# SSD entry of a hybrid trunk layer: the decay clamps' engine, the z gate's buffer, and the places of the gate product and of the later output-weight splits

## The chip, the cores and the metric

The kernel runs on one core of one Trainium2 chip. The metric is the device time of one launch in microseconds (us), the median of three runs. The engines are named as the profile names them: PE is the matrix engine TensorE, with PEld for its weight loads, DVE is VectorE, ACT is ScalarE, POOL is GpSimd, and SP is SyncE, which only issues transfers here.

## What is computed

One layer of a streaming encoder: 1024 tokens, width 1024, all in float32. The normalised input goes through one projection; its columns feed an SSD (Mamba-2) group of 8 heads and an attention group of 8 heads; the two outputs side by side go through the output projection, and a feed-forward block follows. The change touches the SSD group alone:

```python
def ssd_scan(xdt, adt, bm, cm):
    ...
    a_cs = jnp.cumsum(A, axis=2)
    seg = a_cs[:, :, :, None] - a_cs[:, :, None]
    causal = jnp.tril(jnp.ones((L, L), dtype=bool))[:, :, None, None]
    decay_ls = jnp.exp(jnp.where(causal, seg, -jnp.inf))
    cb = jnp.einsum('bclgn,bcsgn->bclsg', Cm, Bm)
    y_diag = jnp.einsum('bclsg,bclsge,bcsgep->bclgep', cb, decay_ls, X)
    ...
def ssd_mixer(z, xbc, dt_raw, conv_w, conv_b, dt_bias, a_log, d_skip, norm_w):
    ...
    y = ssd_scan(xs * dt[..., None], dt * A, bm, cm)
    y = y + d_skip.astype(jnp.float32)[:, None] * xs
    y = y.reshape(b, s, SSD_WIDTH) * jax.nn.silu(z.astype(jnp.float32))
    return rmsnorm(y, norm_w).astype(z.dtype)
```

`seg` is the difference of two running sums, the exponent of a decay. The kernel clamps it at zero before the exponential, so that positions outside the causal triangle, which a mask sets to zero afterwards, cannot overflow. `z` is the gate: its silu multiplies the SSD output.

## The kernel before

**Matrix products.** Every float32 operand of a large product is kept as a high and a low half, and each product is three matmuls (`mm3`, L77 to L79). The halves are made by `split` (L81 to L87): the high half on ScalarE (L83 with a scale, L86 without), then the low half, the operand minus its high half, on VectorE (L84, L87).

**What sets the order.** A scheduler places every instruction in the queue of its engine by its own estimate of time; the engines then work through their queues in order. `tc.issue_after(i)` adds one constraint: what is issued under it comes behind `i` in the queue of `i`'s own engine. It says nothing about other engines. TensorE's order in the SSD loop is written out in this way by `pe` (L706 to L710), which puts each matmul behind the one before it.

**The z projection.** `z_tile` (L640) makes the gate for one tile of 128 tokens, 260 columns at a time; `wz_weights` loads the weights of one pass. The pass `ch == 1` comes first, then `ch == 0` for tiles 0 to 7. In the second pass ScalarE's tanh goes from PSUM into the buffer `zt`, of which there is one (L655), and VectorE's product of that and the PSUM tile goes into `zs` (L656). Tiles 2 to 5 of this pass lie in the two PSUM banks `s`, the others in `acc` and `pv` (named `zps`). `zlast` keeps the tanh and the product of the last tile.

**Output weights.** `wout_split` halves the eight blocks of output weights. Blocks 0 to 3 go into `hth[0]`/`htl[0]` during the second z pass. Blocks 4 to 7 go into `hth[1]`/`htl[1]`, the memory that token tiles 4 to 7 of the layer's normalised input occupy until the z matmuls have read them. Each is scaled by column halves, so four blocks make eight instructions L83 (tile `hH1`) and eight L84 (tile `hL1`). They are issued behind both entries of `pin`.

**The SSD loop.** The 1024 tokens are eight chunks of 128. For each, `ssd_pre` (L712) prepares:
- `xdt` on VectorE (L716) and `xdd` on GpSimd (L717);
- the gate's fine factor, an in-place product on `zs` on GpSimd (L719);
- the decay exponents `cr`, running sums fetched by a transfer from DRAM to all partitions, with two buffers;
- the clamps, one for each head: heads 0 to 3 on ScalarE (L726), heads 4 to 7 on VectorE (L728);
- `cb` on VectorE from TensorE's products (L737), the exponential `th` of four heads on ScalarE (L743), and `th` times `cb` on VectorE (L744).

Chunk 0's share of this is issued during the z pass, behind its tile 0; each later chunk's stands in the iteration of the chunk before it. `ssd_y` (L807) then runs TensorE's products: `ydp` (from `xdt` and `th`), `yop` from the state, and `stp` for the next state; VectorE sums them into `yy` (L832). `ssd_norm` (L838) multiplies `yy` by the gate (L840), squares it on ScalarE (L842), takes the root of the mean on GpSimd (`rstd`, L118), and scales on ScalarE (L844). `ssd_turn` (L846) transposes `yy` on TensorE into `xps`. `wout_half` (L875) runs the output projection (`wops`) of the chunk, part of it between the loop's other steps.

PSUM is handed over when the z pass ends: the pools that hold `s`, `acc` and `pv` close, and `ydp`, `yop`, `stp` (tag `ssd`), `xps` and `wops` open in their banks. Chunk 0's `ydp` gets the bank of z tile 5.

The loop as written:

```python
    for c in range(NT):
        if c == 1:
            ssd_turn(*turn)
        y, t = ssd_y(c, *pre)
        if c > 1:
            ssd_turn(*turn)
        if c == 1:
            at = wout_rhs(0, 1)
        if c > 1:
            ssd_norm(c, y, t)
        turn = (c, y)
        if c < NT - 1:
            pre = ssd_pre(c + 1, x_tile, lambda: wout_half(c, slice(0, 3)))
            if c < 2:
                ssd_norm(c, y, t, at)
            row_scale(pin[0])
            wout_half(c, slice(3, 8))
            if c == 0:
                for j in range(4, 8):
                    pin[:] = zlast
                    wout_split(j, wt[j])
        else:
            wout_half(c)
```

Of the kernel before, what the change touches and what calls it, by code (L numbers as in the profile page):

```python
# [10 lines left out]
F32 = mybir.dt.float32  # L11
# [54 lines left out]
def tile_block(ctx: ExitStack, tc: tile.TileContext, x, crep, pk, w_ada, w_first, w_ft, w_z,  # L66
# [573 lines left out]
    def z_tile(ch, st, wz):  # L640
# [4 lines left out]
        for kt in range(KT):  # L645
            mm3(ps, hth[st // 4][:, st % 4, kt, :], htl[st // 4][:, st % 4, kt, :],
                wz[kt // 2][0][:, kt % 2, :],
                wz[kt // 2][1][:, kt % 2, :], kt == 0, kt == KT - 1)
        nz = 260
        if ch == 1:  # L650
            A.activation(zs[:, st, 260:512], ps[:, 0:252], AF.Silu)
            V.tensor_tensor(zs[:, st, 512:520], ps[:, 252:260], pkt[:, DTB:DTB + 8], ALU.add)
            return
        th = wzp.tile([P, 272], F32, tag="zt", bufs=1, name="zt")
        zlast[:] = [A.activation(th[:, 0:nz], ps[:, 0:nz], AF.Tanh).ins,  # L655
                    V.scalar_tensor_tensor(zs[:, st, ch * 260:ch * 260 + nz], th[:, 0:nz], 1.0, ps[:, 0:nz],  # L656
                                           op0=ALU.add, op1=ALU.mult).ins]

# [53 lines left out]
    def ssd_pre(c, xp_, between=None):  # L712
# [5 lines left out]
        ms_ = []  # L718
        G.tensor_tensor(h8(zs[:, c, 0:512]), h8(zs[:, c, 0:512]), hb("t", c), ALU.mult)  # L719
        cr = bcp.tile([P, 8, P], F32, tag="rm", bufs=2, name="cr")  # L720
        nc.sync.dma_start(cr, rows_from(acd, 8 * c, 8))
        for g in range(2):
            for k in range(4 * g, 4 * g + 4):
                a = acc_[:, 8 * c + k:8 * c + k + 1]
                if g == 0:
                    A.activation(cr[:, k], cr[:, k], AF.Relu, scale=-1.0, bias=a)  # L726
                else:
                    V.tensor_scalar(cr[:, k], cr[:, k], a, 0.0, op0=ALU.subtract, op1=ALU.min)  # L728
            if g == 0:
# [12 lines left out]
            m = th512().rearrange("p (h l) -> p h l", h=4)  # L742
            pin1 = A.activation(m, cr[:, 4 * g:4 * g + 4], AF.Exp, scale=(-1.0, 1.0)[g])  # L743
            pin2 = V.tensor_tensor(m, m, cb[:, g:g + 1, :].to_broadcast([P, 4, P]), ALU.mult)  # L744
            ms_.append(m)
        pin[:] = [pin1.ins, pin2.ins]
        return xdt, xdd, cb, ms_

# [58 lines left out]
    def ssd_y(c, xdt, xdd, cb, ms_):  # L807
# [28 lines left out]
        return y, t  # L836

    def ssd_norm(c, y, t, at=None):  # L838
        with tc.issue_after(at) if at else ExitStack():
            V.tensor_tensor(y, y, zs[:, c, 0:512], ALU.mult)  # L840
        ms = stat()
        A.activation(t, y, AF.Square, accum_out=ms)  # L842
        r = rstd(ms, 512.0 * EPS)
        A.activation(y, y, AF.Copy, scale=r)  # L844
# [93 lines left out]
    for c in range(NT):  # L938
# [10 lines left out]
        if c < NT - 1:  # L949
# [5 lines left out]
            if c == 0:  # L955
                for j in range(4, 8):
                    pin[:] = zlast
                    wout_split(j, wt[j])
# [610 lines left out]
```

## Time and profile before

| | |
|---|---|
| runs | 1210.37, 1210.83, 1214.28 us |
| median | 1210.83 us |
| profiled execution | 1213.89 us |
| its span, first to last instruction | 1212.2 us |
| mean granted TensorE clock | 0.991 |
| PEld, weight loads | 970.0 us busy (80%) |
| DVE | 930.4 us (77%) |
| ACT | 579.5 us (48%) |
| POOL | 159.0 us (13%) |

A row of a timeline gives the start in us from the span's start, the duration, the engine, the line of the kernel, the operation, the tiles written and read, the shape and the count of equal instructions in a row; in brackets stands the wait ahead of it and what ended it. A row of the windows gives the stretch and its length, then the busy time of TensorE (with its number of instructions), weight loads, VectorE, ScalarE and GpSimd, then TensorE's mean granted clock (1.00 is full speed), the DMA engines' share and GB/s. A row of the waits gives the group that waited, the engine, tile and line that released it, the sum, the count and the longest. In the page's chain, each engine's share is that of the chain of work that ended last.

### The profile page before, as it was taken

Reading aid. Unit: us, or ns where it says so; the run is one execution under the profiler, and the core shown is the slowest. Engines: PE = TensorE matmul, PEld = TensorE weight load, DVE = VectorE, ACT = ScalarE, POOL = GpSimd, SP = SyncE. Lnnn points to the kernel's source line nnn. Section 1 sums busy time; section 2 is a strip of 40 time slices with the busy share of each in tenths; the row PEclk is TensorE's granted clock in tenths of the full one; section 3 lists DMA queues with packets and bytes.
Section 4 is the critical chain, followed back from the end, with each engine's and each line's share of the span. In section 5 each row is a group of like instructions: output and inputs, shape, how many; then the busy total and the mean of one; then the engine's idle time right before and its main releaser. Section 6 shows DMA issues by size and latency. Waiting matters only on the chain.

```text
span 1212.2 us, 15576 instructions
## 1 busy us (share of the span) xinstructions
PE 1161.0 (96%) x5767; PEld 970.0 (80%) x5767; DVE 930.4 (77%) x1418; ACT 579.5 (48%) x938; POOL 159.0 (13%) x182
## 2 busy tenths in 40 slices
PE   4998999989999989999999999999999999999996
PEld 3877787878879978888788888888888888888885
DVE  6846455686596888747999988898889779766986
ACT  4536455673243556476544543345334445433454
POOL 1202232441000255300000000000000000000522
PEclk9999999999999989999999999999999999999999
DMA  9722121311477313141123223322233278733443
GB/s 338 254 59 81 40 64 46 96 73 53 151 255 254 124 36 111 55 148 53 72 102 122 98 107 109 131 78 84 99 131 113 87 269 283 264 116 128 155 132 147
DMA packets 57803, 155.09 MB, mean 128 GB/s; under 512 B 5808, under 2 KB 6016, under 8 KB 56320
## 3 DMA queue, kind: packets, MB, share of 16 engines
q1 hardware_dynamic: 50672, 129.73, 31.4%
q10 hardware_dynamic: 7056, 24.38, 5.1%
q8 instruction: 45, 0.74, 0.2%
q14 instruction: 30, 0.25, 0.1%
HBM read 121.28 MB, written 28.61 MB: 124 GB/s over the span
## 4 chain that ended last, share of the span: by engine, by line
PE 65%; DVE 7%; DMA 2%; ACT 2%; issue 1%; POOL 1%; POOLq 0%; SPq 0%; ACTq 0%; DVEq 0%
PE dn L79 5%; PE dn L78 5%; PE dn L77 5%; PE uY L77 5%; PE uY L79 5%; PE uY L78 5%; PE wops L708 4%; PE uX L79 3%; PE uZ L78 3%; PE uX L77 3%; PE uX L78 3%; PE uZ L77 3%; PE uZ L79 3%; PE s L77 2%; PE s L78 2%; PE s L79 2%
## 5 line engine op out<-in xcount | busy, mean ns | idle before, releaser
L78 PE MATMUL dn<-w 128*128 128x512 f32 x296 | 108.1, 392 | 0.0
L77 PE MATMUL dn<-w 128*128 128x512 f32 x296 | 108.1, 391 | 0.0
L79 PE MATMUL dn<-w 128*128 128x512 f32 x296 | 100.2, 391 | 0.2 <-DVE w L87 0.2
L77 PE MATMUL uY<-tH,w 128*128 128x512 f32 x248 | 97.2, 392 | 0.0
L78 PE MATMUL uY<-tL,w 128*128 128x512 f32 x248 | 97.0, 391 | 0.0
L79 PE MATMUL uY<-tH,w 128*128 128x512 f32 x248 | 96.9, 391 | 0.0
L1430 POOL TENSOR_TENSOR ya<-ya,xs 128x512 f32<-128x512 f32 x4 | 17.2, 4334 | 557.7 <-ACT xs L1426 557.7
L86 ACT ACTIVATE w<-ya 128x1024 fp32r<-128x1024 f32 (+1 forms) x41 | 39.2, 956 | 87.5 <-PE uY L79 84.2
L708 PE MATMUL wops<-hH,yhl 128*128 128x512 f32 x224 | 72.9, 398 | 0.0
L79 PEld LDWEIGHTS dn<-w 128*128 128x128 f32 x296 | 55.4, 188 | 13.2 <-DVE w L87 1.1
L77 PEld LDWEIGHTS dn<-w 128*128 128x128 f32 x296 | 55.5, 188 | 12.4
L78 PEld LDWEIGHTS dn<-w 128*128 128x128 f32 x296 | 55.5, 188 | 12.2
L409 DVE CUSTOM_DVE_ANT_0 p<-s,bias 128x640 f32<-128x640 f32 (+4 forms) x64 | 40.6, 652 | 25.7 <-PE tp L441 10.6
L86 ACT ACTIVATE w<-xs 128x1024 fp32r<-128x1024 f32 (+1 forms) x41 | 39.1, 954 | 38.0 <-PE uY L79 33.3
L415 POOL TENSOR_SCALAR p<-p,st 128x640 f32<-128x640 f32 (+4 forms) x64 | 45.9, 723 | 76.9 <-DVE st L414 66.7
L87 DVE TENSOR_TENSOR pt<-tp,pt 128x512 fp32r<-128x512 f32 (+2 forms) x72 | 42.1, 596 | 17.0 <-ACT pt L86 16.5
L79 PEld LDWEIGHTS uY<-tH,w 128*128 128x128 f32 x248 | 46.5, 188 | 10.4
L77 PEld LDWEIGHTS uY<-tH,w 128*128 128x128 f32 x248 | 46.5, 188 | 10.3
L78 PEld LDWEIGHTS uY<-tL,w 128*128 128x128 f32 x248 | 46.6, 188 | 10.2
L77 PE MATMUL s<-hH,wh 128*128 128x512 f32 x128 | 50.2, 392 | 1.7 <-DVE ct L516 1.7
L1104 DVE SCALAR_TENSOR_TENSOR a<-cv,pkt,a 128x1023 f32<-128x1023 f32 (+1 forms) x40 | 51.1, 1280 | 0.1
L412 ACT ACTIVATE p<-p,st 128x640 f32<-128x640 f32 (+4 forms) x64 | 44.1, 690 | 14.0 <-DVE st L409 13.8
(463 smaller groups left out, 3405.6 us busy)
## 6 DMA issues: line engine op xcount, KB each, us to landing
wos<-in_w_ada_dram SPq DMA_DIRECT2D x25, 512.0 KB, 4.5
gz<-a ACTq DMA_DIRECT2D x10, 1024.0 KB, 5.1
ya<-in_w_up_dram SPq DMA_DIRECT2D x11, 768.0 KB, 4.1
xs<-in_w_up_dram SPq DMA_DIRECT2D x11, 768.0 KB, 4.1
adat<-in_w_ada_dram SPq DMA_DIRECT2D x16, 512.0 KB, 5.8
raws<-in_w_ft_dram SPq DMA_DIRECT2D x14, 512.0 KB, 3.7
gy<-a ACTq DMA_DIRECT2D x10, 512.0 KB, 2.6
qk<-in_x_dram SPq DMA_DIRECT2D x8, 512.0 KB, 7.2
```

Source lines behind the costliest of these rows:

```text
L77: T.matmul(ps, lh, rh, start=start, stop=False, skip_group_check=more)
L78: T.matmul(ps, lh, rl, start=False, stop=False, skip_group_check=more)
L79: T.matmul(ps, ll, rh, start=False, stop=stop, skip_group_check=more)
L86: i = A.activation(hi, src, AF.Copy) if ehi is A else ehi.tensor_copy(hi, src)
L87: return i, elo.tensor_tensor(lo, src, f32(hi), ALU.subtract)
L409: V.tensor_tensor_reduce(out=dst, in0=src, in1=bsl, scale=-1.0, scalar=3e38, op0=ALU.add, op1=ALU.min, accum_out=nm)
L412: A.activation(pv_, pv_, AF.Exp, scale=-1.0, bias=nm, accum_out=rs)
L415: G.tensor_scalar(pv_, pv_, rr, 1.0, op0=ALU.mult, op1=ALU.mult)
L708: i = op(*a, **k)
L1104: V.scalar_tensor_tensor(a[:, j:S], c[:, 0:S - j], w[2 - j], a[:, j:S], op0=ALU.mult, op1=ALU.add)
L1430: G.tensor_tensor(src, src, fnr[:, halves[1]], ALU.mult)
```

## The change

Five things change, all in what `z_tile`, `ssd_pre`, `ssd_norm` and the loop issue.

- The clamps of heads 4 to 7 go to ScalarE with those of heads 0 to 3. They were the minimum of a difference and zero and are now the rectified negative difference, so the sign of their exponential's scale changes with them.
- In the second z pass tanh writes into `zs` itself and the product works there in place; the buffer `zt` is gone. `zlast` holds the product alone.
- The gate's fine product moves from ahead of the clamps to the end of `ssd_pre`, behind the second exponential.
- `ssd_norm` records the gate's product (L840 before) in `gated`.
- Blocks 4 to 7 of the output weights are split behind `zlast` and `gated`. Both entries are VectorE instructions; before, one was the tanh on ScalarE.

```diff
--- before.py
+++ after.py
@@ -646,15 +646,13 @@
             mm3(ps, hth[st // 4][:, st % 4, kt, :], htl[st // 4][:, st % 4, kt, :],
                 wz[kt // 2][0][:, kt % 2, :],
                 wz[kt // 2][1][:, kt % 2, :], kt == 0, kt == KT - 1)
-        nz = 260
         if ch == 1:
             A.activation(zs[:, st, 260:512], ps[:, 0:252], AF.Silu)
             V.tensor_tensor(zs[:, st, 512:520], ps[:, 252:260], pkt[:, DTB:DTB + 8], ALU.add)
             return
-        th = wzp.tile([P, 272], F32, tag="zt", bufs=1, name="zt")
-        zlast[:] = [A.activation(th[:, 0:nz], ps[:, 0:nz], AF.Tanh).ins,
-                    V.scalar_tensor_tensor(zs[:, st, ch * 260:ch * 260 + nz], th[:, 0:nz], 1.0, ps[:, 0:nz],
-                                           op0=ALU.add, op1=ALU.mult).ins]
+        z = zs[:, st, 0:260]
+        A.activation(z, ps[:, 0:260], AF.Tanh)
+        zlast[:] = [V.scalar_tensor_tensor(z, z, 1.0, ps[:, 0:260], op0=ALU.add, op1=ALU.mult).ins]
 
     def dt_prep():
         dtr = zs[:, :, 512:520]
@@ -716,16 +714,12 @@
         V.tensor_tensor(h8(xdt), h8(xs[:, c, :]), hb("dt", c), ALU.mult)
         G.tensor_tensor(h8(xdd), h8(xdt), hb("de", c), ALU.mult)
         ms_ = []
-        G.tensor_tensor(h8(zs[:, c, 0:512]), h8(zs[:, c, 0:512]), hb("t", c), ALU.mult)
         cr = bcp.tile([P, 8, P], F32, tag="rm", bufs=2, name="cr")
         nc.sync.dma_start(cr, rows_from(acd, 8 * c, 8))
         for g in range(2):
             for k in range(4 * g, 4 * g + 4):
                 a = acc_[:, 8 * c + k:8 * c + k + 1]
-                if g == 0:
-                    A.activation(cr[:, k], cr[:, k], AF.Relu, scale=-1.0, bias=a)
-                else:
-                    V.tensor_scalar(cr[:, k], cr[:, k], a, 0.0, op0=ALU.subtract, op1=ALU.min)
+                A.activation(cr[:, k], cr[:, k], AF.Relu, scale=-1.0, bias=a)
             if g == 0:
                 cbp = xp_()
                 for i in range(2):
@@ -740,10 +734,12 @@
                 if between:
                     between()
             m = th512().rearrange("p (h l) -> p h l", h=4)
-            pin1 = A.activation(m, cr[:, 4 * g:4 * g + 4], AF.Exp, scale=(-1.0, 1.0)[g])
+            pin1 = A.activation(m, cr[:, 4 * g:4 * g + 4], AF.Exp, scale=-1.0)
             pin2 = V.tensor_tensor(m, m, cb[:, g:g + 1, :].to_broadcast([P, 4, P]), ALU.mult)
             ms_.append(m)
         pin[:] = [pin1.ins, pin2.ins]
+        with tc.issue_after(pin1.ins):
+            G.tensor_tensor(h8(zs[:, c, 0:512]), h8(zs[:, c, 0:512]), hb("t", c), ALU.mult)
         return xdt, xdd, cb, ms_
 
     wz = wz_weights(1)
@@ -835,9 +831,11 @@
             V.tensor_tensor(y, y, t, ALU.add)
         return y, t
 
+    gated = []
+
     def ssd_norm(c, y, t, at=None):
         with tc.issue_after(at) if at else ExitStack():
-            V.tensor_tensor(y, y, zs[:, c, 0:512], ALU.mult)
+            gated[:] = [V.tensor_tensor(y, y, zs[:, c, 0:512], ALU.mult).ins]
         ms = stat()
         A.activation(t, y, AF.Square, accum_out=ms)
         r = rstd(ms, 512.0 * EPS)
@@ -954,7 +952,7 @@
             wout_half(c, slice(3, 8))
             if c == 0:
                 for j in range(4, 8):
-                    pin[:] = zlast
+                    pin[:] = zlast + gated
                     wout_split(j, wt[j])
         else:
             wout_half(c)
```

The changed kernel's lines stand one to four above those of before in this region (L655 is L654, L656 is L655, L726 is L722, L743 is L737, L840 is L838). Three places of the queues follow; the words after an arrow are tiles, with the scheduler's numbers.

ScalarE's queue at the end of the z pass, before (`s_3951` is z tile 5, `zps_4007` tile 7; `cr_4206` is chunk 2's, `cr_4309` chunk 3's):

```order
L655 ACTIVATE zt_3948<-s_3923 128x260
L726 ACTIVATE cr_4206<-cr_4206,acc_2862 128x128 x4
L655 ACTIVATE zt_3976<-s_3951 128x260
L655 ACTIVATE zt_4004<-zps_3979 128x260
L655 ACTIVATE zt_4032<-zps_4007 128x260
L83 ACTIVATE hH1_84<-wos_2866,pkt_66 128x512 x2
L743 ACTIVATE th_4123<-cr_4094 128x512
L83 ACTIVATE hH1_84<-wos_2866,pkt_66 128x512 x2
L83 ACTIVATE hH1_84<-raws_68,pkt_66 128x512 x2
L83 ACTIVATE hH1_84<-wos_2866,pkt_66 128x512 x2
L743 ACTIVATE th_4130<-cr_4094 128x512
```

and as built after the change (`s_3946` is z tile 5, `zps_4000` tile 7; `cr_4085` is chunk 1's):

```order
L83 ACTIVATE hH1_84<-raws_68,pkt_66 128x512
L722 ACTIVATE cr_4085<-cr_4085,acc_2862 128x128 x6
L737 ACTIVATE th_3817<-cr_3804 128x512
L690 ACTIVATE ex3_2863<-tp_3785 128x128
L654 ACTIVATE zs_2856<-zps_3973 128x260
L722 ACTIVATE cr_4085<-cr_4085,acc_2862 128x128
L737 ACTIVATE th_3824<-cr_3804 128x512
L722 ACTIVATE cr_4085<-cr_4085,acc_2862 128x128
L83 ACTIVATE hH1_84<-raws_68,pkt_66 128x512
L83 ACTIVATE hH1_84<-wos_2866,pkt_66 128x512 x4
L654 ACTIVATE zs_2856<-s_3946 128x260
L654 ACTIVATE zs_2856<-zps_4000 128x260
```

All eight L83 stood behind the last tanh; they now stand ahead of the tanh of z tile 5: five of them next to it, one in the first row here and two above these rows. VectorE's queue from the last products of z to chunk 1's second `th`, before:

```order
L656 SCALAR_TENSOR_TENSOR zs_2856<-zt_4032,zps_4007 128x260
L716 TENSOR_TENSOR xdt_4201<-xs_2842,sm_dt_2861 128x512
L84 SCALAR_TENSOR_TENSOR hL1_86<-wos_2866,pkt_66,hH1_84 128x512 x2
L832 TENSOR_TENSOR yy_4081<-ydp_4072,yy_4081 128x512
L737 TENSOR_TENSOR cb_4105<-xps_4100,tle1_2864 128x512
L84 SCALAR_TENSOR_TENSOR hL1_86<-wos_2866,pkt_66,hH1_84 128x512 x2
L840 TENSOR_TENSOR yy_4081<-yy_4081,zs_2856 128x512
L84 SCALAR_TENSOR_TENSOR hL1_86<-raws_68,pkt_66,hH1_84 128x512
L744 TENSOR_TENSOR th_4123<-th_4123,cb_4105 128x512
L84 SCALAR_TENSOR_TENSOR hL1_86<-raws_68,pkt_66,hH1_84 128x512
L84 SCALAR_TENSOR_TENSOR hL1_86<-wos_2866,pkt_66,hH1_84 128x512 x2
L744 TENSOR_TENSOR th_4130<-th_4130,cb_4105 128x512
```

and after:

```order
L655 SCALAR_TENSOR_TENSOR zs_2856<-zs_2856,zps_4000 128x260
L828 TENSOR_TENSOR yy_4073<-ydp_4064,yy_4073 128x512
L714 TENSOR_TENSOR xdt_4193<-xs_2842,sm_dt_2861 128x512
L838 TENSOR_TENSOR yy_4073<-yy_4073,zs_2856 128x512
L84 SCALAR_TENSOR_TENSOR hL1_86<-wos_2866,pkt_66,hH1_84 128x512 x4
L84 SCALAR_TENSOR_TENSOR hL1_86<-raws_68,pkt_66,hH1_84 128x512 x2
L84 SCALAR_TENSOR_TENSOR hL1_86<-wos_2866,pkt_66,hH1_84 128x512 x2
L731 TENSOR_TENSOR cb_4096<-xps_4091,tle1_2864 128x512
L738 TENSOR_TENSOR th_4114<-th_4114,cb_4096 128x512
L738 TENSOR_TENSOR th_4121<-th_4121,cb_4096 128x512
```

The gate's product stood behind four L84 and chunk 1's `cb`; it now stands ahead of all eight L84, and these ahead of `cb`.

## The prediction

> **What bounds the kernel now.** I read the page first, then the waits of TensorE, then the windows round its longest wait, then the timelines of VectorE, ScalarE and GpSimd there.
>
> ```profile
> PE 1161.0 (96%) x5767; PEld 970.0 (80%) x5767; DVE 930.4 (77%) x1418; ACT 579.5 (48%) x938; POOL 159.0 (13%) x182
> PE 65%; DVE 7%; DMA 2%; ACT 2%; issue 1%; POOL 1%; POOLq 0%; SPq 0%; ACTq 0%; DVEq 0%
> ...
> PE ydp L708 <- DVE zs L656: 5.4, 1, 5.4
> PE xps L708 <- ACT yy L844: 1.6, 2, 1.3
> PE ydp L708 <- DVE th L744: 1.0, 1, 1.0
> PE s L77 <- DVE zs L656: 0.3, 1, 0.3
> ...
> 408.00:420.00 12.00, 11.66 (x98) 11.46 (x97) 9.99 (x15) 9.34 (x23) 6.05 (x4) 1.00 0.39 135
> 420.00:430.00 10.00, 4.64 (x32) 4.43 (x31) 8.85 (x18) 3.25 (x10) 7.16 (x6) 0.75 0.15 54
> 430.00:440.00 10.00, 10.00 (x42) 8.70 (x42) 8.16 (x11) 6.44 (x12) 6.40 (x7) 0.74 0.14 52
> 440.00:450.00 10.00, 8.73 (x53) 7.49 (x52) 9.78 (x16) 5.15 (x13) 4.21 (x5) 1.00 0.16 54
> ```
>
> TensorE is busy for 96% of the span, so only its waits and its clock can be won. The four waits are those of the entry of the SSD stage (400 to 530 us); they sum to 8.3 us. In the columns of the windows (TensorE, weight loads, VectorE, ScalarE, GpSimd, clock) TensorE works 4.64 of 10 us in the worst one, while VectorE works 8.85 and ScalarE 3.25: VectorE is the late engine. The mean clock there is 0.75.
>
> ```profile
> 422.42 0.28 PE L79 MATMUL s<-wzh,hL 128*128 128x260 f32 x1
> 428.06 3.68 PE L708 MATMUL ydp<-xdt,th 128*128 128x64 f32 x16 [5.36 <-DVE zs L656]
> 431.52 2.02 PE L708 MATMUL stp<-xdd,cb 128*128 128x256 f32 x4
> ...
> 442.34 1.90 PE L708 MATMUL ydp<-xdt,th 128*128 128x64 f32 x16
> ...
> 425.00:426.00 1.00, 0.00 (x0) 0.00 (x0) 1.00 (x2) 0.30 (x1) 1.00 (x2) 0.52 0.00 0
> 435.00:436.00 1.00, 1.00 (x5) 0.82 (x4) 1.00 (x2) 0.72 (x2) 0.22 (x2) 0.86 0.00 0
> ```
>
> The last z matmul ends at 422.70; chunk 0's ydp starts at 428.06 and takes 3.68 us where chunk 1's takes 1.90: the granted clock is at half from 425 to 435.
>
> ```profile
> 417.51 1.65 DVE L728 TENSOR_SCALAR cr<-cr,acc 128x128 f32<-128x128 f32 x4
> 424.41 0.41 DVE L656 SCALAR_TENSOR_TENSOR zs<-zt,s 128x260 f32<-128x260 f32 x1
> 424.74 2.92 DVE L728 TENSOR_SCALAR cr<-cr,acc 128x128 f32<-128x128 f32 x4
> 427.59 0.41 DVE L656 SCALAR_TENSOR_TENSOR zs<-zt,s 128x260 f32<-128x260 f32 x1
> ```
>
> ydp takes over the PSUM bank of z tile 5, so it waits for that tile's product on VectorE (427.59 to 428.00). Ahead of it stand four clamps that took 2.92 us beside GpSimd, and its tanh had to wait for the single zt buffer.
>
> **The change part by part.** *Clamps.* 32 clamps leave VectorE, 32 join ScalarE's 32.
>
> ```profile
> 414.34 2.52 ACT L726 ACTIVATE cr<-cr,acc 128x128 f32<-128x128 f32 x8 [0.81 <-DMA cr<-acd]
> 416.77 0.62 ACT L743 ACTIVATE th<-cr 128x512 f32<-128x512 f32 x1
> 419.74 0.37 ACT L655 ACTIVATE zt<-s 128x260 f32<-128x260 f32 x1
> 429.20 1.32 ACT L83 ACTIVATE hH<-wos,pkt 128x512 fp32r<-128x512 f32 x2
> ```
>
> One costs ScalarE 0.305 us (2.43 us from the first to the exp, over 8), 1.2 us more a chunk; ScalarE has the room (5 to 6.4 busy of 10). On VectorE four cost 0.8 us alone and up to 2.92 beside GpSimd.
>
> *z in place.* Tanh and product cost the same; the wait for zt goes. z tile 4's product then leaves 1.57 us of clamps behind it too, so the last z GEMM starts without its 0.3 us wait and TensorE runs dry at 422.4.
>
> *High halves.* The eight L83 were held behind the last tanh. They are held now by two VectorE instructions, which order nothing on ScalarE, and the built order puts all eight ahead of z tile 5's tanh. This is the part that bites. ScalarE's queue from the rows (each instruction 0.1 us under its duration, since the next begins that much before its end): L83 and yhl until 414; eight clamps from the landing at 414.34 to 416.8; L83, tanh 4, L83 (0.61, 0.3, 0.61) to 418.3; six clamps to 420.15; exp 0.52, the small exp 0.13, tanh 6 0.3, clamp 0.3, exp 0.52, clamp 0.3 to 422.25; five L83 of 0.61 to 425.3; tanh 5 to 425.7; VectorE's product 0.42; ydp at **426.2**. So its start moves up by 1.85 us, not by 5.36: 3.05 us of the gap are the five L83. Bounds: with 0.1 us more at each of the ten changes of kind ydp comes at 427.2; with all L83 gone it would come at 423.2.
>
> *Gate product.* Eight products on GpSimd before and after. The order it is given is on ScalarE's queue and holds nothing on GpSimd: five still stand first, three move behind the two xdd and yy. No wait of TensorE hangs on them; price nothing, hidden behind the gap; without this cover 1.03 us each.
>
> *Low halves behind the gate.*
>
> ```profile
> 432.59 2.97 DVE L84 SCALAR_TENSOR_TENSOR hL<-wos,pkt,hH 128x512 fp32r<-128x512 f32 x2
> 436.69 1.40 DVE L84 SCALAR_TENSOR_TENSOR hL<-wos,pkt,hH 128x512 fp32r<-128x512 f32 x2
> 438.01 0.68 DVE L840 TENSOR_TENSOR yy<-yy,zs 128x512 f32<-128x512 f32 x1
> ...
> 432.08 1.49 POOL L719 TENSOR_TENSOR zs<-zs,sm_t 128x512 f32<-128x512 f32 x1
> 433.63 1.39 POOL L717 TENSOR_TENSOR xdd<-xdt,ex 128x512 f32<-128x512 f32 x1
> ...
> 441.07 0.72 ACT L844 ACTIVATE yy<-yy,st 128x512 f32<-128x512 f32 x1 [1.55 <-POOL st L118]
> ```
>
> Before, two L84 beside GpSimd took 2.97 us, two alone 1.40 (0.66 each in the queue); four of them stood ahead of the gate, and the gate's chain (square, rstd, L844) let TensorE wait 1.27 us. Now all eight stand behind the gate and ahead of chunk 1's cb and th. With the clock still at half, ydp ends by 429.9 (3.46 us from ydp to stp, and 0.2); yy, xdt and the gate take 1.8 us alone, 3.0 with GpSimd's queue between: 431.7 to 432.9. L844 follows by 437.6 even behind chunk 3's eight clamps (its cr is asked for at 430.5, lands 3.9 us later, 2.5 us of clamps, 0.7), while TensorE reaches its transposes at 438.1 with the clock back at the first wops and at 439.4 with the clock back at 435.3 as before:
>
> ```profile
> 434.48 0.78 PE L708 MATMUL wops<-hH,yhl 128*128 128x512 f32 x1
> ...
> 488.98 5.45 PE wops L708 x24
> ```
>
> 6.4 us from ydp's start to the first wops, then 5.45 for its 24 (2.7 us of them at half speed add 1.3). So the wait on L844 goes. But eight L84, two of them beside GpSimd's two products, take 2.97 + 6 x 0.66 = 6.9 us (5.3 alone): 437.0 to 439.8; cb and th 1.2: chunk 1's ydp can start between 438.2 and 441.0, and TensorE is there by 439.9. I take 441.0, since GpSimd's queue is full there: **1.3 us** earlier than 442.34. Bounds 2.4, and -0.4 with four L84 slowed (2 x 2.97 + 4 x 0.66 = 8.6 us, ydp at 442.7).
>
> The rows say that VectorE and GpSimd take turns at something. The Trainium skill, GPSIMD Engine Reference, section 1 Specifications, says that their SBUF interfaces are shared, with contention for a VectorE instruction with two SBUF inputs. It speaks against this change: L84 has two, the z product (one operand in PSUM) has one. By the rule eight L84 pay for the two products that run beside them, an estimate of 5.3 + 2 x 1.03 = 7.4 us against my 6.9, and ydp at 441.5.
>
> *Later chunks.* TensorE's order is the same but for one matmul. The two waits left:
>
> ```profile
> 456.08 0.66 PE L708 MATMUL xps<-ident,yy 128*128 128x128 f32 x4 [0.30 <-ACT yy L844]
> 484.09 2.00 PE L708 MATMUL ydp<-xdt,th 128*128 128x64 f32 x16 [1.00 <-DVE th L744]
> 482.58 0.86 DVE L728 TENSOR_SCALAR cr<-cr,acc 128x128 f32<-128x128 f32 x4
> ```
>
> The second had 0.78 us of clamps just ahead of th, which go; I give it 0.8 and the first 0.3. From 530 us on the orders are equal; nothing is won or lost there.
>
> **Sum.** 1.3 + 0.8 + 0.3 = 2.4 us. The profiled execution took 1213.9 us (span 1212.2 and 1.7 around it), so one like it would take 1211.5. The median before is 3.1 us under that execution; against 1210.83 it is **1208.4 us**. A difference of 0.3% is 3.6 us, about what a measurement of this kernel tells from none: the forecast lies within it.
>
> **Rivals.** *The gap closes further.* If TensorE keeps its clock through the 3.8 us gap, ydp takes 1.90 us instead of 3.68, the gate comes 1.8 us earlier, TensorE is through its wops by 436, and chunk 1's ydp starts at 441.0 - 1.8 = 439.2, or 438.7 with half of GpSimd's 1.0 us turn saved: 3.6 us earlier; with the 1.1 of the later chunks 4.7 us: 1206.1. For it: the gap is 1.5 us shorter. Against: the clock fell at 425.0, 2.3 us after the last matmul. The Trainium skill, TensorE: Matmul & The Clock Gate, Part 1, says the clock drops after an idle window of about 3.4 us that runs freely; by it a whole idle window fits a gap of 3.8 us in about one execution of eight, so most would stay warm. The trace disagrees in part: here a window about a third busy was enough. Chance 0.33.
>
> *ScalarE becomes the late engine (slower).* In each chunk eight clamps wait for cr's landing, and square and L844 stand behind them.
>
> ```profile
> DMA to landing us min/median/max: 3.4/3.9/5.1
> ...
> 485.35 0.72 ACT L844 ACTIVATE yy<-yy,st 128x512 f32<-128x512 f32 x1 [1.83 <-POOL st L118]
> 487.71 0.60 PE L708 MATMUL xps<-ident,yy 128*128 128x128 f32 x4
> ```
>
> L844 ended 1.64 us before its transposes there, so the four clamps' 1.2 us fit. If cr lands 5.1 us after its issue instead of 3.9, L844 comes 2.4 us later: 0.8 late in each of five chunks, and 2.7 in chunk 1's turn, which had no slack: 6.7 us lost, 2.4 won: 1215.1. It decides from 1.64 us of delay. Against: the order asks for cr a chunk early. Chance 0.15.
>
> *Nothing arrives.* Four L84 slowed take back all of ydp's gain, as in the bound above, and of the later waits 0.4 us goes: 1210.8. For it: GpSimd's queue; against: only two of its products fall there. Chance 0.08.
>
> **Chances.** Forecast 0.44, its own range 1206.8 to 1210.5; about a sixth of it lies beyond 0.3%. Faster 0.33 + 0.07 = 0.40; same 0.37 + 0.08 = 0.45; slower 0.15. Range 1205.0 to 1213.5: below, the clock rival and its 1.1 us of spread; above, the nothing case and the upper runs before.
>
> **What will show it.** Right: ydp's wait on the z product 3.5 to 4.3 us with five L83 just ahead of tanh 5; no wait on L844 at the first transposes; a wait of 1 to 2 us of chunk 1's ydp on th, behind eight L84; no wait near 484. Wrong: a clock of 1.00 all through 420 to 440 (the first rival); L844 after the transposes' turn in several chunks (the second); a ydp that starts before 424, which would mean that the splits did not hold tanh 5.

## The result, and the profile after

| | before | the change |
|---|---|---|
| median of 22 runs | 1211.49 us | 1209.47 us |
| lowest to highest | 1210.24 to 1214.28 | 1207.20 to 1212.72 |
| profiled execution, its span | 1213.89, 1212.2 us | 1207.34, 1205.6 us |

The ratio is 0.9975, with a 95% interval of 0.9967 to 0.9983: the change takes 2.1 to 4.0 us off, 3.0 in the middle. The two medians lie only 2.0 us apart, and in a later comparison on one chip the ratio was 0.9984 (0.9969 to 0.9999), 1.9 us; so the size is known to about a microsecond. The forecast was 1208.4 us, from a median before of 1210.83; 2.4 us off the median of 22 runs would be 1209.1.

The two profiled executions are 6.6 us of span apart, which is twice 3.0. So the first thing to read is where they part. Two stretches of the windows view, long ahead of the changed code, in before, in the change, and in a second profile of the change (stretch, length, busy TensorE, weight loads, VectorE, ScalarE, GpSimd, clock, DMA share, GB/s):

```profile
119.00:125.00 6.00, 4.84 (x14) 3.82 (x15) 3.37 (x10) 3.25 (x9) 3.31 (x8) 0.72 0.35 111
238.00:245.00 7.00, 5.74 (x33) 5.19 (x34) 4.71 (x16) 4.94 (x14) 3.84 (x7) 0.76 1.01 395
```

```profile
119.00:125.00 6.00, 5.68 (x28) 4.80 (x29) 2.13 (x7) 2.02 (x5) 2.97 (x7) 1.00 0.22 76
238.00:245.00 7.00, 6.19 (x46) 5.49 (x47) 4.99 (x20) 5.23 (x17) 2.62 (x8) 1.00 0.61 243
```

```profile
119.00:125.00 6.00, 5.27 (x16) 4.24 (x17) 2.54 (x7) 2.43 (x6) 2.93 (x7) 0.72 0.26 100
238.00:245.00 7.00, 5.70 (x33) 5.15 (x34) 4.66 (x16) 4.91 (x15) 3.13 (x7) 0.76 0.93 375
```

In before and in the second profile of the change, the clock was at half for 3.41 us near 121 us and again near 240 us; in the change's first profile it was not. The second profile has a span of 1208.8 us, 3.2 more than the first, and the code is the same. So some 3.2 of the 6.6 us come and go between executions of the same code, and spans of single executions cannot be compared. What can be compared is the stretch that the change touches. I take the **entry time**: from the first matmul `tp<-sm_e` inside the z pass to chunk 7's first `ydp`. Its two ends in the timeline of TensorE and the stretch between them in the windows, before and then after:

```profile
415.49 0.33 PE L691 MATMUL tp<-sm_e,sgt 128*128 128x64 f32 x2
504.38 0.89 PE L708 MATMUL ydp<-xdt,th 128*128 128x64 f32 x7
415.49:504.38 88.89, 80.62 (x455) 70.33 (x454) 77.56 (x133) 48.67 (x111) 46.96 (x46) 0.94 0.22 78
```

```profile
411.89 0.33 PE L689 MATMUL tp<-sm_e,sgt 128*128 128x64 f32 x2
497.82 0.55 PE L706 MATMUL ydp<-xdt,th 128*128 128x64 f32 x4
411.89:497.82 85.93, 80.77 (x454) 70.97 (x453) 71.72 (x101) 58.26 (x143) 45.67 (x46) 0.94 0.24 80
```

88.89 us became 85.93: 2.96 us, as much as the ratio of the run times says (3.0). (The second profile of the change has 85.77.) From chunk 5's `ydp` on, the same matmuls stand 6.5 to 6.6 us apart in the two profiles to the end, and at the entry's start 3.60. TensorE works the same 80.7 us; its idle time fell from 8.27 to 5.16. VectorE's work fell by 5.8 us, ScalarE's rose by 9.6.

What is left of the idle time in the change, by the timelines of TensorE, ScalarE and VectorE (before a row's bracket: start, duration, engine, line, operation, tiles, shape, count):

```profile
418.18 0.28 PE L79 MATMUL zps<-wzh,hL 128*128 128x260 f32 x1
422.62 3.67 PE L706 MATMUL ydp<-xdt,th 128*128 128x64 f32 x16 [4.16 <-DVE zs L655]
...
435.54 0.60 PE L706 MATMUL xps<-ident,yy 128*128 128x128 f32 x4
436.80 1.10 PE L706 MATMUL ydp<-xdt,th 128*128 128x64 f32 x8 [0.66 <-DVE th L738]
438.25 1.10 PE L706 MATMUL ydp<-xdt,th 128*128 128x64 f32 x8 [0.34 <-DVE th L738]
...
477.51 2.00 PE L706 MATMUL ydp<-xdt,th 128*128 128x64 f32 x16
```

```profile
419.28 2.55 ACT L83 ACTIVATE hH<-wos,pkt 128x512 fp32r<-128x512 f32 x4
421.73 0.37 ACT L654 ACTIVATE zs<-s 128x260 f32<-128x260 f32 x1
```

```profile
420.00 1.41 DVE L738 TENSOR_TENSOR th<-th,cb 128x512 f32<-128x512 f32 x1
422.14 0.43 DVE L655 SCALAR_TENSOR_TENSOR zs<-zs,s 128x260 f32<-128x260 f32 x1 [0.72 <-ACT zs L654]
...
428.39 4.30 DVE L84 SCALAR_TENSOR_TENSOR hL<-wos,pkt,hH 128x512 fp32r<-128x512 f32 x4
432.62 1.40 DVE L84 SCALAR_TENSOR_TENSOR hL<-raws,pkt,hH 128x512 fp32r<-128x512 f32 x2
433.94 1.40 DVE L84 SCALAR_TENSOR_TENSOR hL<-wos,pkt,hH 128x512 fp32r<-128x512 f32 x2
435.27 0.68 DVE L731 TENSOR_TENSOR cb<-xps,tle 128x512 f32<-128x512 f32 x1
```

Chunk 0's `ydp` waits 4.16 us in place of 5.36, the transposes (`xps<-ident,yy`) wait no more, chunk 1's `ydp` waits twice, 1.00 us in all, and the wait of chunk 5's `ydp` (before at 484, now at 477.51) is gone. One row already says that the prediction read too much into the L83: VectorE waited for tile 5's tanh for 0.72 us only. Until 421.4 it was itself at work.

### The profile page after: what moved, and what is told of

It reads as the page before. It is cut to its first block, busy times and chain, and to the rows that moved or that the text cites. A ratio compares the mean times of both kernels' runs of the same rounds, so it can differ in the third digit from the quotient of the medians.

```text
span 1205.6 us, 15575 instructions
## 1 busy us (share of the span) xinstructions
PE 1157.8 (96%) x5767; PEld 967.9 (80%) x5767; DVE 924.3 (77%) x1386; ACT 589.6 (49%) x970; POOL 158.0 (13%) x182
## 4 chain that ended last, share of the span: by engine, by line
PE 68%; DVE 6%; DMA 2%; ACT 1%; issue 1%; POOL 0%; POOLq 0%; SPq 0%; DVEq 0%; ACTq 0%
PE wops L706 6%; PE dn L79 5%; PE dn L77 5%; PE dn L78 5%; PE uY L77 5%; PE uY L79 5%; PE uY L78 5%; PE uX L79 3%; PE uX L77 3%; PE uZ L78 3%; PE uZ L77 3%; PE uX L78 3%; PE uZ L79 3%; PE s L78 2%; PE s L77 2%; PE s L79 2%
## 5 line engine op out<-in xcount | busy, mean ns | idle before, releaser
L87 DVE TENSOR_TENSOR pt<-tp,pt 128x512 fp32r<-128x512 f32 (+2 forms) x72 | 42.1, 596 | 16.1 <-ACT pt L86 15.6
```

The source lines that it names most:

```text
L87: return i, elo.tensor_tensor(lo, src, f32(hi), ALU.subtract)
```

## The experiments

Eleven more kernels, and the changed one once more, were profiled and timed against the kernel before. The table gives the entry time, TensorE's idle time within it, how long TensorE worked at half clock within it, and what is left when the idle time and half of that work are taken off. The ratio is that of the run times to the runs of before on the same chip, with its 95% interval.

| kernel | ratio (95%) | entry | idle | at half clock | left |
|---|---|---|---|---|---|
| before | 1 | 88.89 | 8.27 | 7.24 | 77.0 |
| the change | 0.9975 (0.9967 to 0.9983) | 85.93 | 5.16 | 8.46 | 76.5 |
| the_change_again | 0.9984 (0.9969 to 0.9999) | 85.77 | 5.10 | 8.51 | 76.4 |
| clamps_alone | 1.0019 (1.0007 to 1.0032) | 90.31 | 8.21 | 11.76 | 76.2 |
| gated_alone | 1.0019 (1.0008 to 1.0031) | 91.35 | 9.53 | 10.20 | 76.7 |
| z_in_place_alone | 1.0046 (1.0032 to 1.0061) | 94.69 | 15.11 | 6.23 | 76.5 |
| clamps_and_gated | 0.9987 (0.9977 to 0.9997) | 87.16 | 5.69 | 10.25 | 76.3 |
| change_without_gated | 0.9986 (0.9974 to 0.9998) | 88.26 | 6.98 | 10.24 | 76.2 |
| high_halves_behind_tanh | 0.9986 (0.9971 to 1.0001) | 89.28 | 6.59 | 12.58 | 76.4 |
| gate_product_on_its_queue | 0.9992 (0.9980 to 1.0003) | 88.54 | 6.44 | 10.24 | 77.0 |
| gate_product_on_its_queue_before | 0.9992 (0.9978 to 1.0006) | 86.62 | 6.07 | 6.83 | 77.1 |
| both_holds | 0.9966 (0.9952 to 0.9980) | 84.53 | 4.00 | 6.83 | 77.1 |
| both_holds_two_early_two_late | 0.9961 (0.9948 to 0.9974) | 83.12 | 4.53 | 3.41 | 76.9 |
| both_holds_one_low_half_later | 0.9947 (0.9930 to 0.9965) | 82.54 | 3.40 | 3.41 | 77.4 |

The last column hardly moves (76.2 to 77.4). So two things make nearly all of these differences: how long TensorE waits, and how much it does at half clock afterwards. The half-clock stretches come in multiples of 3.41 us.

### The parts alone

**The clamps alone**, on the kernel before:

```diff
-                if g == 0:
-                    A.activation(cr[:, k], cr[:, k], AF.Relu, scale=-1.0, bias=a)
-                else:
-                    V.tensor_scalar(cr[:, k], cr[:, k], a, 0.0, op0=ALU.subtract, op1=ALU.min)
+                A.activation(cr[:, k], cr[:, k], AF.Relu, scale=-1.0, bias=a)
...
-            pin1 = A.activation(m, cr[:, 4 * g:4 * g + 4], AF.Exp, scale=(-1.0, 1.0)[g])
+            pin1 = A.activation(m, cr[:, 4 * g:4 * g + 4], AF.Exp, scale=-1.0)
```

> The kernel before with only the clamps of heads 4 to 7 moved to ScalarE. Theory B (what bounds chunk 0's ydp is VectorE's queue ahead of z tile 5's product): the four clamps of 2.92 us leave it, but zt still has one buffer, so tile 5's tanh waits for tile 4's product and the product for the tanh, 0.9 us in a row; ydp's wait falls from 5.36 to 3 to 4.5 us. The later wait of 1.0 us (ydp of the sixth chunk on th, four clamps just ahead) goes. The first transposes keep their wait of about 1.3 us or more, since four L84 and more stand ahead of the gate as before. Entry time 85.5 to 87.5 us from 88.89; if it stays at 88 or more the clamps were not what made VectorE late.

Its timeline of TensorE (two rows) and of VectorE (four) show one wait closed and another opened:

```profile
423.52 2.42 PE L708 MATMUL ydp<-xdt,th 128*128 128x64 f32 x16 [1.97 <-DVE zs L656]
440.47 1.12 PE L708 MATMUL xps<-ident,yy 128*128 128x128 f32 x4 [6.24 <-ACT yy L841]
```

```profile
427.90 2.97 DVE L84 SCALAR_TENSOR_TENSOR hL<-wos,pkt,hH 128x512 fp32r<-128x512 f32 x2
...
432.00 2.80 DVE L84 SCALAR_TENSOR_TENSOR hL<-wos,pkt,hH 128x512 fp32r<-128x512 f32 x2
...
435.32 0.74 DVE L84 SCALAR_TENSOR_TENSOR hL<-raws,pkt,hH 128x512 fp32r<-128x512 f32 x1
435.98 0.68 DVE L837 TENSOR_TENSOR yy<-yy,zs 128x512 f32<-128x512 f32 x1
```

`ydp` waits 1.97 us, less than I gave it (3 to 4.5): the clamps were what made VectorE late. But the kernel is slower, not faster: the entry is 90.31 us, where 85.5 to 87.5 was expected. TensorE comes earlier to the first transposes, and five L84, 6.5 us in all, still stand ahead of the gate (L837): a wait of 6.24 us with 10.24 us at half clock behind it, after 3.41 us at half clock behind the first wait. The entry time was therefore a bad sign for what made VectorE late; the first wait alone shows it. Of the later waits on `th` none is left, as expected.

**The hold behind the gate alone**, on the kernel before (`gated` recorded as in the change, the tanh kept as the other pin):

```diff
-                    pin[:] = zlast
+                    pin[:] = [zlast[0]] + gated
```

> The kernel before with only the low halves of the later output weights held behind chunk 0's gate (high halves behind the last tanh, as before). ydp's wait stays at 5.3 us. The first transposes' wait on L844 (1.27 us) goes, since no L84 stands ahead of the gate; but chunk 1's ydp then waits for its second th, behind all eight L84 (some 6.9 us): 1 to 2 us. The wait of 1.0 us in the sixth chunk stays. Entry time 88 to 89.5 us: no difference that can be measured. If the hold by itself is what pays, it falls to 87 us or less.

```profile
427.27 3.67 PE L708 MATMUL ydp<-xdt,th 128*128 128x64 f32 x16 [5.36 <-DVE zs L656]
443.51 1.27 PE L708 MATMUL ydp<-xdt,th 128*128 128x64 f32 x8 [2.64 <-DVE th L744]
```

In TensorE's timeline the wait at the transposes is gone, as expected, and chunk 1's second half of `ydp` waits 2.64 us behind eight L84. The entry is 2.5 us longer, more than I expected: TensorE is idle for 1.3 us more, and a further 3.41 us at half clock follow that wait. Alone it costs 0.19%.

**z in place alone**, on the kernel before:

```diff
-        th = wzp.tile([P, 272], F32, tag="zt", bufs=1, name="zt")
-        zlast[:] = [A.activation(th[:, 0:nz], ps[:, 0:nz], AF.Tanh).ins,
...
+        z = zs[:, st, 0:260]
+        zlast[:] = [A.activation(z, ps[:, 0:260], AF.Tanh).ins,
+                    V.scalar_tensor_tensor(z, z, 1.0, ps[:, 0:260], op0=ALU.add, op1=ALU.mult).ins]
```

> The kernel before with only the z tiles finished in place. The built order then puts the tanh of z tile 5 behind all eight L83 and its product behind all eight L84 and four clamps, because the last z tile issued (7) is done ahead of tile 5. By the reading that whatever stands ahead of tile 5's product sets chunk 0's ydp, the eight L84 and the clamps (eight at 0.66 to 1.5 us and 2.9 us) add 8 to 12 us: ydp's wait is 13 to 17 us in place of 5.36, the wait of 1.27 us at the first transposes goes, and the entry time is 95 to 100 us in place of 88.89, the kernel 0.5 to 0.9% slower. If ydp waits 6 us or less, the product of tile 5 is not what holds it.

```profile
432.43 3.68 PE L706 MATMUL ydp<-xdt,th 128*128 128x64 f32 x16 [14.28 <-DVE zs L655]
```

```profile
422.25 2.64 DVE L84 SCALAR_TENSOR_TENSOR hL<-wos,pkt,hH 128x512 fp32r<-128x512 f32 x2
424.81 3.26 DVE L726 TENSOR_SCALAR cr<-cr,acc 128x128 f32<-128x128 f32 x4
427.99 1.40 DVE L84 SCALAR_TENSOR_TENSOR hL<-raws,pkt,hH 128x512 fp32r<-128x512 f32 x2
429.31 2.72 DVE L84 SCALAR_TENSOR_TENSOR hL<-wos,pkt,hH 128x512 fp32r<-128x512 f32 x4
431.96 0.41 DVE L655 SCALAR_TENSOR_TENSOR zs<-zs,s 128x260 f32<-128x260 f32 x1
```

TensorE's row and VectorE's queue: tile 5's product stands behind eight L84 and four clamps, `ydp` waits 14.28 us, and the kernel is 0.46% slower. This is the clearest sign that what stands ahead of that one product sets the entry. The buffer `zt` had a use: without it the scheduler was free to finish tile 7 first, and the pin is on tile 7, not on tile 5, whose bank `ydp` needs. (0.46% is a little under the 0.5 to 0.9 expected; 10.8 of the 17.07 us at half clock fell into the wait itself, where TensorE had nothing to lose.)

**Clamps and hold together**, `zt` kept (the two diffs above in one kernel):

> The kernel before with the clamps on ScalarE and the low halves behind the gate, but with the buffer zt kept and the high halves behind the last tanh. Alone, each of the two made the kernel slower: clamps_alone cut ydp's wait to 1.97 us and paid 6.24 at the first transposes (L84 ahead of the gate), gated_alone kept 5.36 at ydp and paid 2.64 on chunk 1's th. If the two only pay together, ydp's wait stays near 2 us, the transposes' wait falls from 6.24 to 1.5 or less, chunk 1's ydp waits some 3 us for its second th, and the entry time is 85.5 to 89 us, at or under the kernel before (88.89). If z in place is the part that pays, it is 90 us or more, as in clamps_alone (90.31).

`ydp`'s wait was 1.97 us, the transposes' 1.03, chunk 1's second half of `ydp` 2.70; entry 87.16 us, ratio 0.9987. Two edits that cost 0.19% each alone gain 0.13% together, without z in place. The clamps shorten the first wait, and the hold keeps the gate's chain from taking its place.

**The change without the hold** (high and low halves behind the last tanh and product):

```diff
-                    pin[:] = zlast + gated
+                    pin[:] = zlast
```

> The changed kernel with the later output weights split behind the last tanh and the last z product, as before, in place of behind the gate (high and low halves). In the changed kernel VectorE stood idle for 3.5 us while ydp ran and then put eight L84 ahead of chunk 1's cb and th. Without the hold three L84 run in that idle time. To be compared with high_halves_behind_tanh, which has the hold and is else the same (ydp's wait 3.35, then 3.15 us of waiting on chunk 1's th). If the hold helps, this kernel is slower than that one: the first transposes wait over 1 us for the gate's chain and the entry time is 90 us or more. If it hurts, chunk 1's ydp waits 1 us or less for th and the entry time is 86 to 88.

`zlast` has the tanh again here, as in the next kernel. Neither of the two expected outcomes came out whole: the transposes did wait for the gate's chain, 3.64 us, but chunk 1's `ydp` did not wait at all, and the entry time was 88.26 against 89.28. Between these two kernels the times (0.9986 both) tell nothing. So with clamps and z in place already there, the hold moves a wait of 3.1 to 3.6 us from one place to the next.

### What holds tile 5's product

> The changed kernel with the eight high halves of the later output weights (L83) held behind the last tanh on ScalarE again, the low halves behind the gate as in the change. I look at the wait of chunk 0's ydp (4.16 us in the changed kernel) and at the entry time, from the first matmul tp<-sm_e inside the z pass to chunk 7's first ydp (88.89 us before, 85.93 us after). Theory A, the prediction's bound: five L83 of 0.61 us hold the tanh of z tile 5, so without them ydp's wait falls by about 3.05 us to 1.1, and the entry time to 83 us or less. Theory B: VectorE's own queue is nearly as late as ScalarE's. In the changed kernel VectorE worked without a gap from 408 us until its product on tile 5 and waited 0.72 us for that tanh; so the wait falls only to about 3.4 us, the entry time to about 85.2, and the time of the kernel by 0.7 us, which can hardly be measured.

```diff
-        A.activation(z, ps[:, 0:260], AF.Tanh)
-        zlast[:] = [V.scalar_tensor_tensor(z, z, 1.0, ps[:, 0:260], op0=ALU.add, op1=ALU.mult).ins]
+        zlast[:] = [A.activation(z, ps[:, 0:260], AF.Tanh).ins,
+                    V.scalar_tensor_tensor(z, z, 1.0, ps[:, 0:260], op0=ALU.add, op1=ALU.mult).ins]
...
-                    pin[:] = zlast + gated
+                    pin[:] = [zlast[0]] + gated
```

ScalarE's, VectorE's and TensorE's timelines:

```profile
420.82 0.39 ACT L654 ACTIVATE zs<-s 128x260 f32<-128x260 f32 x1 [0.75 <-PE s L79]
```

```profile
422.44 1.41 DVE L738 TENSOR_TENSOR th<-th,cb 128x512 f32<-128x512 f32 x1
423.78 0.41 DVE L655 SCALAR_TENSOR_TENSOR zs<-zs,s 128x260 f32<-128x260 f32 x1
```

```profile
424.25 3.67 PE L706 MATMUL ydp<-xdt,th 128*128 128x64 f32 x16 [3.34 <-DVE zs L655]
439.67 3.17 PE L706 MATMUL ydp<-xdt,th 128*128 128x64 f32 x16 [3.15 <-DVE th L738]
```

The tanh is done at 421.2, and the product starts 2.6 us later, right behind VectorE's previous instruction. The wait is 3.34 us: theory B to the tenth. The rest of its expectation failed. The entry was not 85.2 but 89.28, because chunk 1's `ydp`, which needs VectorE's `th`, can start no sooner: 25.3 us after the entry's start, 24.9 in the change. TensorE, earlier by 0.8 us and at full clock for longer, waits 3.15 us for it and then works 6.83 us at half clock.

The gate's fine product is the other half of that. In the change it is ordered behind an instruction of ScalarE; taken back to its old place the five engines' queues are the same row by row, and so they are when it alone is moved in the kernel before. It moves nothing. On GpSimd's own queue the order binds:

```diff
-        G.tensor_tensor(h8(xdd), h8(xdt), hb("de", c), ALU.mult)
+        pin0_ = G.tensor_tensor(h8(xdd), h8(xdt), hb("de", c), ALU.mult)
...
-        with tc.issue_after(pin1.ins):
+        with tc.issue_after(pin0_.ins):
             G.tensor_tensor(h8(zs[:, c, 0:512]), h8(zs[:, c, 0:512]), hb("t", c), ALU.mult)
```

> The changed kernel with the gate's fine product held behind its own chunk's xdd on GpSimd's queue, so that GpSimd has nothing to do beside VectorE from 409 to 419 us, where the changed kernel ran five of these products. Both theories expect ydp's wait near 4.1 us, since the five L83 still hold tile 5's tanh on ScalarE. Theory B (VectorE and GpSimd take turns) expects VectorE's two L87 of 128x1024 there at about 1.2 us instead of 2.06, and a wait of VectorE for the tanh of 3 us in place of 0.72. If instead these two L87 stay at 2 us, it is not GpSimd that slows them. The price of the move: each gate product now runs beside later VectorE work, up to 1 us for each, so the entry time may come out anywhere from 85 to 88 us.

VectorE in the change, and then with this edit:

```profile
409.98 2.06 DVE L87 TENSOR_TENSOR hL<-wos,hH 128x1024 fp32r<-128x1024 f32 x1
411.97 2.06 DVE L87 TENSOR_TENSOR hL<-raws,hH 128x1024 fp32r<-128x1024 f32 x1
```

```profile
410.42 1.22 DVE L87 TENSOR_TENSOR hL<-wos,hH 128x1024 fp32r<-128x1024 f32 x1
411.55 1.22 DVE L87 TENSOR_TENSOR hL<-raws,hH 128x1024 fp32r<-128x1024 f32 x1
...
422.68 0.42 DVE L655 SCALAR_TENSOR_TENSOR zs<-zs,s 128x260 f32<-128x260 f32 x1 [2.37 <-ACT zs L654]
```

The same instruction takes 1.22 us without GpSimd beside it and 2.06 with it, and VectorE now waits 2.37 us for tile 5's tanh. `ydp`'s wait is 4.26 us, as both theories said: the L83 hold it by themselves. The entry, 88.54 us, is above the 85 to 88 that were expected and 2.6 longer than in the change: chunk 1's `ydp` waits 1.79 us for `th`, and 3.41 us at half clock follow.

> Both edits together: high halves behind the last tanh, and the gate's product behind xdd on GpSimd's queue. Theory A (the L83 alone set ydp): the same as high_halves_behind_tanh within 0.3 us. Theory B (ScalarE's and VectorE's queues are both late, one close behind the other): ydp's wait falls to about 1 us, from 4.16 less 0.72 for the L83 less some 2.6 for VectorE (two L87 of 2.06 at 1.2, th times cb of 1.41 at 0.68, xdt and small products beside). Then the granted clock decides the rest: if it stays at 1.00 through so short a gap, ydp takes 1.9 us instead of 3.67 and the entry time goes to 80 to 82 us, the kernel to 4 to 5 us under the changed one; if it falls as before, the entry time is about 83.

TensorE's timeline with both edits:

```profile
423.21 2.23 PE L706 MATMUL ydp<-xdt,th 128*128 128x64 f32 x16 [1.12 <-DVE zs L655]
435.57 0.66 PE L706 MATMUL xps<-ident,yy 128*128 128x128 f32 x4 [1.64 <-ACT yy L842]
437.31 2.64 PE L706 MATMUL ydp<-xdt,th 128*128 128x64 f32 x16 [1.08 <-DVE th L738]
```

`ydp` waits 1.12 us: theory B. Each of the two queues had hidden the other: moving the L83 alone takes 0.8 us off the wait, moving GpSimd's products alone nothing, both together 3.0. The entry, 84.53 us, is longer than either case of the expectation: one stretch of 3.41 us at half clock at `ydp` and one at chunk 1, and a wait of 1.64 us at the transposes for the gate's chain, which no theory had.

> The kernel before, with only the gate's fine product held behind its chunk's xdd on GpSimd's queue. If GpSimd beside it is what made VectorE late there, the four clamps ahead of z tile 5's product take 0.8 us instead of 2.92 and the two L87 1.2 instead of about 2; ydp's wait falls from 5.36 to 1 to 2 us, and the entry time from 88.89 to 85 to 86 us or less. If the turns are only moved to later chunks, the wait falls and the entry time stays at 88 to 89.

This is the same edit on the kernel before. Its L87 take 1.22 us too, but the four clamps ahead of tile 5's product took 3.39 us, not 0.8: GpSimd's first products now run beside those. `ydp` waits 3.49 us. The entry is 2.3 us shorter, between the two outcomes that were expected, and the ratio of 0.9992 (0.9978 to 1.0006) shows no difference. The turns are partly saved and partly moved.

### Two further versions

> both_holds with the two low halves of the last weight block (slot 7) behind chunk 1's second th. There, chunk 1's ydp waited 1.08 us for th behind eight L84, and the window with that wait was followed by 3.4 us at half clock. Two L84 fewer, 1.3 us, ahead of th: the wait falls to 0.2 us or less; if the clock then stays up, the entry time falls from 84.53 to 81.5 to 82.5 us, if not, to about 83.5. If a wait for slot 7's low half appears in chunk 1's output products (near 446 us) the gain is gone.

The edit against both_holds:

```diff
             pre = ssd_pre(c + 1, x_tile, lambda: wout_half(c, slice(0, 3)))
+            th_ = pin[1]
...
-                    pin[:] = [zlast[0]] + gated
+                    pin[:] = [zlast[0], gated[0] if j < 7 else th_]
```

TensorE's timeline, and the windows of its entry:

```profile
420.84 2.38 PE L706 MATMUL ydp<-xdt,th 128*128 128x64 f32 x16 [1.25 <-DVE zs L655]
433.07 0.66 PE L706 MATMUL xps<-ident,yy 128*128 128x128 f32 x4 [1.50 <-ACT yy L842]
433.62 2.00 PE L706 MATMUL ydp<-xdt,th 128*128 128x64 f32 x16
...
413.02:495.56 82.54, 79.14 (x454) 68.48 (x452) 70.38 (x100) 56.60 (x144) 46.07 (x46) 0.98 0.24 78
```

The wait of 1.08 us on `th` is gone, the clock stays up from 425.70 to the entry's end, and no wait on the last weight block (slot 7) appears. The median of its 6 runs is 1205.59 us, the ratio 0.9947 (0.9930 to 0.9965). Its interval lies wholly under that of the change run beside it; with that of both_holds it overlaps.

> both_holds with the low halves of slot 4 behind the last z product only, so that they run while VectorE waits for ydp, those of slot 5 behind the gate, and those of slots 6 and 7 behind chunk 1's second th. Two L84 stand ahead of yy, two between the gate and th, four behind. The wait of 1.08 us on th goes, the gate is not later unless GpSimd's products beside make the first two L84 slow (up to 3 us in place of 1.4, which still fits in VectorE's idle stretch of 2 to 3 us). Entry time 81.5 to 83.5 us from 84.53. Against it: slots 6 and 7 may come too late for chunk 1's output products: up to 1.2 us.

The edit against both_holds, with the same `th_`:

```diff
-                    pin[:] = [zlast[0]] + gated
+                    pin[:] = [zlast[0], zlast[1] if j < 5 else gated[0] if j < 6 else th_]
```

The entry is 83.12 us, as expected, and the ratio 0.9961. Chunk 1's `th` is not waited for, but the transposes wait 3.44 us for the gate's chain, twice as long as in both_holds. Here too the wait that was taken away came back one step earlier. The two versions' intervals overlap.

> The changed kernel once more, beside the three others on one chip. Its queues are the same, so the waits of the entry should be as in its first profile (4.2 us at ydp, 1.0 at chunk 1's th), within 0.3 us. If half-clock stretches are a matter of where the waits fall and not of the code alone, their number and place differ from the first profile (one of 10.24 us, none outside the SSD entry), and the entry time with them by 1.7 us for each 3.41 us at half clock in which TensorE is busy: 84 to 89 us.

The waits were 4.09, 0.67 and 0.34 us, and the entry had the same half-clock stretch of 10.24 us. So within the entry this second profile repeats the first to 0.2 us (85.77 and 85.93), and its half-clock stretch stands at the same place; what differs between the two executions are the stretches near 121 and 240 us. Two profiles cannot say how often that happens.

## Why the prediction was right, and where it was not

- **The bound.** VectorE's lateness at the entry was the right thing to read: the whole gain lies between the entry's start and chunk 5's `ydp`.
- **ydp 1.85 us earlier.** It comes 10.73 us after the entry's start in place of 12.57: 1.84. The working of ScalarE's queue held in its parts too: from the first of eight clamps to the next instruction 2.37 us (2.43 reckoned), and the tanh behind five L83 starts 9.84 us after the entry's start (9.8 reckoned).
- **"3.05 us of the gap are the five L83"**, and the bound "with all L83 gone it would come at 423.2". This failed. Without them the wait falls by 0.8 us, not 3.05, as VectorE was itself busy until 0.72 us before it could take up that product in the change. I had followed ScalarE's queue to its end and not VectorE's own, with its L87 at 2.06 us beside GpSimd. The forecast was spared by luck: the later of two near-equal queues was the one that I had counted.
- **Gate product at nothing.** Right, and for the reason given: the queues do not change.
- **Eight L84 in 6.9 us, chunk 1's ydp 1.3 us earlier.** From 428.39 to 435.27 they took 6.88 us, though differently made up (four slowed to 4.30, four at 2.8, where I had two slowed to 2.97); that the sums agree is luck. Chunk 1's `ydp` starts 1.94 us ahead, but stops after half of its matmuls for the second `th`. By chunk 2's `ydp`, which starts 36.51 us after the entry's start before and 35.23 now, the change is 1.28 us ahead. The transposes' wait went, and the wait on `th` was 1.00 us, at the lower edge of "1 to 2 us".
- **Later chunks.** Forecast 0.3 and 0.8; measured 0.60 by the fourth `ydp` (47.22 and 45.34 us after the start) and 1.10 by the sixth (68.60 and 65.62). I had sized both by one wait or a part of it, and each is 0.3 us more. For the second, the whole wait of 1.00 us went, not 0.8. Taken from 1210.83, the sum of 2.96 instead of 2.4 lies within the forecast's own range of times.
- **The clock rival.** It did not happen in either profile of the change: 10.24 us at half clock, as before. It needs a shorter wait than I gave it: in other kernels, waits of 1.1 to 2.0 us at `ydp` had 3.41 to 6.83 us behind them, waits of 3.3 to 4.3 us 3.41 to 10.24, and only one of 0.91 us (both_holds_two_early_two_late) had none. By the counts in the last part of this document, an estimate: a gap of 4.16 us leaves at least one window of 3.41 us with 2.08 us idle, so with 1.33 us of work or less, wherever the windows fall, and every window with so little work was followed by half clock. For such a gap the chance of 0.33 was too high.
- **ScalarE as the late engine.** It did not happen in the change. A trace of it is in the two versions of the last section of the experiments, where one clamp waited 2.4 us for `cr` just ahead of L842. GpSimd's root, which L842 needs, was done 0.3 and 0.4 us before L842 started, so the clamp held it by no more than that.
- **Nothing arrives.** Its condition was met, four L84 were slowed, but to 1.07 us each and not 1.49: the eight took 6.88 us, not 8.6.

## What to carry to other kernels

A wait that is closed shows the next one. The clamps alone took 3.4 us off the first wait and put 5.0 on the second; the hold alone closed a wait of 1.27 us and opened one of 2.64; together they paid. Before pricing the removal of what stands ahead of an instruction, follow every engine that it waits for to the same instant; the gain is the distance to the second-latest. And an ordering constraint is worth checking in the built queues. On ScalarE's queue the one on the gate product did nothing. On GpSimd's queue it lengthened the changed kernel's entry by 2.6 us when set alone, and took 4.7 us off it (89.28 to 84.53) where the high halves were also held; of these two kernels' run times the intervals overlap.

## What the runs showed of the hardware

TensorE's clock goes to half in stretches of 3.41 us and multiples (6.82, 10.24, 17.07), and a wait much shorter than that can start one. In both_holds (windows view, the window ahead of its half-clock stretch, and the stretch):

```profile
421.41:424.83 3.42, 2.30 (x21) 2.09 (x19) 2.08 (x4) 2.83 (x6) 3.42 (x4) 1.00 0.48 153
...
424.83:428.25 3.42, 3.42 (x15) 3.06 (x14) 1.42 (x2) 3.42 (x8) 3.42 (x4) 0.50 0.02 5
```

TensorE worked 2.30 of 3.42 us there, with one wait of 1.12. The Trainium skill, TensorE: Matmul & The Clock Gate, Part 1, has the clock drop after an idle window of about 3.4 us; the length agrees with these stretches, the need for a whole idle window does not. How much work is enough can be bounded. I took 60 to 1190 us of all fourteen traces in windows of 3.41 us, laid so that the clock's changes fall on their edges. Of the windows at full clock, all 15 in which TensorE worked less than 1.46 us were followed by half clock, 27 of the 78 between 1.46 and 2.30 us, and none of the 4480 above 2.30. So a wait of 1.12 us can start a drop and the 1.27 us at the transposes of the kernel before did not; what decides in between stays open.

Four L84 beside GpSimd took 4.30 us, 1.07 each, and four of them alone 2.8. With GpSimd's products moved away (gate_product_on_its_queue against the change) an L87 of 128x1024 fell from 2.06 to 1.22 us and a product of 128x64 (L693) from 1.08 to 0.22. The instructions need not read two tensors: four clamps, which read one tensor and one value per partition, took 0.87 us with GpSimd idle and 3.39 beside it (gate_product_on_its_queue_before). GpSimd is slowed too: a product that takes it 1.03 us took up to 1.49 beside VectorE. That the two engines take turns, one instruction waiting for the other's, fits these numbers; no run isolates it.
